# A hybrid diffusion layer: the second feed-forward product's operands pair by pair, context stores on GpSimd's queue, late residuals, and last sums of squares on TensorE

## The chip, the cores and the metric

The kernel runs on one core of one Trainium2 chip. The metric is the device time of one execution in microseconds (us). TensorE multiplies matrices; VectorE, ScalarE and GpSimd work on tiles elementwise; SyncE issues most of the DMAs. TensorE runs at one of two granted clocks, 1.2 or 2.4 GHz, which the profile shows as .50 and 1.00.

## The reference

One layer of a diffusion trunk with 256 context tokens and 1024 latent tokens, of width 1024, then a last RMSNorm. Three token mixers (a chunked state space scan, a spatial gate, a complex diagonal scan) are followed by the feed-forward part, which is the part that the change touches:

```
h = rmsnorm(x, norm1_g) * (1 + scale1) + shift1
x = x + gate1 * (concat(mixers(h @ w_in)) @ w_out)
h = rmsnorm(x, norm2_g) * (1 + scale2) + shift2                  # the "second norm"
x = x + gate2 * (square(relu(h @ ffn_w1)) @ ffn_w2)              # first and second product
y = rmsnorm(x, final_norm_g)                                     # the "last norm"
```

It is done for the context with modulation `c_ctx` and for the latents with `c`. `ffn_w1` is 1024 x 4096, `ffn_w2` 4096 x 1024, all in float32.

## The kernel before

Activations lie with features on partitions and tokens in columns: columns 0 to 255 are the context, 256 to 1279 the latents. A float32 factor is split into a high part (rounded, by ScalarE) and a low part (the rest, by VectorE), and a product is three matmuls: high x high, high x low, low x high. In the second product those are lines L1405, L1406, L1407 (`mm2`). Helpers record their own lines: L48 is every DMA, L54 every elementwise operation of two tiles, L57 every scalar-tensor-tensor operation, L60 every activation, L201 the passes with a vector of ones that sum squares over partitions, L206 the passes that spread the result.

The 4096 hidden features are 16 pairs of 256. In the first product, pairs are worked off one by one; the context's part of the last four pairs (12 to 15) is done alone at the end (`ctx_pair`): 24 matmuls of 128x256 for each of two halves, relu and square by ScalarE into `cc`, and a store to `ac_d` that ScalarE's queue issues. The latents' activations were stored to `a_d` before.

The second product then runs over groups of pairs: (0-3), (4-7), (8, 9), (10-13). It is a scheme of seven block products (`seven(i, ...)`, in the order 1, 2, 5, 6, 3, 7, 4) for the latents, and four context products `ctx2` between them. A `seven` fills four PSUM banks of tag "w" (five exist), 12 matmuls of 128x512 for each of four pairs: 48 by four banks, bank after bank. Its operands: `uA` is a weight block (from `h0`/`h1`, loads of `ffn_w2`, or from `cb`, a sum of weight blocks that GpSimd makes), `uB` an activation block (from `tb`, a load of `a_d`); `ch` and `cl` are the parts of the context activations `rc`. `tb`, `rc`, `cb` and `xt` share one ring "tm" of ten tiles. `flush` puts a bank into `X` or adds it, the last group also folds the seven X tiles into X2 to X5, which become the four quarters of the result, and applies `residual`: load `xt`, the residual stream, and y = gate x y + xt. `cacc` holds the context's sum and gets its residual likewise.

Pairs 14 and 15 come last, in `last_block` for columns 768, 1024, 256, 512, 0 in this order: eight row blocks, each 12 matmuls of 128x256 in a bank of "w", and then y = gate x bank + y by VectorE. After each block but the first, `final_norm` of the block before runs, and the one of columns 0 to 255 stands at the very end.

The order of instructions on each engine is fixed when the program is built, by a scheduler that simulates times; DMAs are issued by SyncE's queue in that order, but for the stores to `ac_d`. A DMA also waits for the one eight before it in a rotation of semaphores that SyncE's and ScalarE's DMAs share.

## Time and profile before

| | |
|---|---|
| median of 3 runs | 1550.88 us (1548.78 to 1554.53) |
| the profiled execution | 1554.11 us |
| its span, first to last instruction | 1552.3 us |
| mean granted clock of TensorE | .951 |

All times of single instructions below are us from the start of the span of the profiled execution. A row of the timeline gives start, duration, engine, line, operation, output and inputs, shape, the number of like instructions merged into it, and in brackets the idle time of the engine before it and what ended that. Matmuls overlap in the pipeline, so their pace is read from the distance of their starts, not from their durations.

### The profile page before, as it was taken

The numbers are of one execution on the slowest core, as the hardware profiler recorded it, in microseconds if no ns is written. First come the engines' busy times: TensorE is split into PE (matmuls) and PEld (weight loads), VectorE is DVE, ScalarE is ACT, GpSimd is POOL, SyncE is SP. The second block draws the span as 40 slices with busy tenths as digits, with TensorE's granted clock in tenths as the row PEclk, the third lists the DMA queues.
The fourth block names the chain that finished last, engine by engine and source line by source line (L and its number), as shares of the span: only waits on it lengthen the run. The fifth ranks groups of instructions, "written<-read, shape, count | busy, mean of one in ns | idle before, by whom it ended". The sixth has DMA issues, their size and how long they took to land.

```text
span 1552.3 us, 23665 instructions
## 1 busy us (share of the span) xinstructions
PE 1416.1 (91%) x8360; PEld 1198.5 (77%) x8360; DVE 1040.4 (67%) x1772; ACT 713.1 (46%) x1459; POOL 448.6 (29%) x527
## 2 busy tenths in 40 slices
PE   4689898899896799989999999999899999999795
PEld 3567677778774588778888888888788888887795
DVE  5773358766757854758877756574655678879945
ACT  3643434355734633447555545455555243323322
POOL 4555556734635512312000000000331403032033
PEclk9699899999998889989999999999999999999897
DMA  9758785275878874346444444345653245316312
GB/s 318 254 172 257 217 284 186 88 182 153 242 199 242 241 248 126 102 137 200 140 148 147 146 138 139 117 153 176 213 183 115 80 150 175 108 55 193 107 41 97
DMA packets 244747, 258.62 MB, mean 167 GB/s; under 512 B 16212, under 2 KB 168980, under 8 KB 244628
## 3 DMA queue, kind: packets, MB, share of 16 engines
q1 hardware_dynamic: 228724, 239.84, 50.0%
q10 hardware_dynamic: 15904, 17.27, 3.5%
q8 instruction: 66, 1.08, 0.3%
q14 instruction: 53, 0.43, 0.1%
HBM read 188.07 MB, written 68.98 MB: 166 GB/s over the span
## 4 chain that ended last, share of the span: by engine, by line
PE 63%; DVE 8%; DMA 5%; issue 3%; POOL 2%; ACT 2%; SPq 0%; DVEq 0%; ACTq 0%; POOLq 0%
PE ps_w L1251 7%; PE ps_w L1249 7%; PE ps_w L1250 7%; PE ps_w L1405 6%; PE ps_w L1406 6%; PE ps_w L1407 6%; PE ps_mm L222 5%; PE ps_mm L220 5%; PE ps_mm L221 5%; DVE X L54 2%; PE ps_mm L1406 1%; PE ps_mm L1407 1%; PE ps_mm L1405 1%; DVE uA L54 1%; POOL Ht L54 1%
## 5 line engine op out<-in xcount | busy, mean ns | idle before, releaser
L220 PE MATMUL ps_mm<-hi,wh 128*128 128x512 f32 (+1 forms) x576 | 212.6, 369 | 14.9 <-DVE dtr L708 14.5
L221 PE MATMUL ps_mm<-lo,wh 128*128 128x512 f32 (+1 forms) x576 | 211.5, 367 | 0.0
L222 PE MATMUL ps_mm<-hi,wl 128*128 128x512 f32 (+1 forms) x576 | 210.1, 365 | 0.9 <-DVE wl L54 0.9
L1406 PE MATMUL ps_w<-uB,uA 128*128 128x512 f32 (+1 forms) x520 | 191.4, 369 | 8.9 <-DVE uB L54 8.9
L1405 PE MATMUL ps_w<-uB,uA 128*128 128x512 f32 (+1 forms) x520 | 190.8, 371 | 9.0 <-ACT uB L60 8.9
L1407 PE MATMUL ps_w<-uB,uA 128*128 128x512 f32 (+1 forms) x520 | 190.5, 367 | 0.0
L54 POOL TENSOR_TENSOR cb<-h 128x512 f32<-128x512 f32 x14 | 21.7, 1559 | 513.8 <-DMA h<-w 435.1
L220 PEld LDWEIGHTS ps_mm<-hi,wh 128*128 128x128 f32 x576 | 112.2, 195 | 32.2 <-DVE dtr L708 15.3
L222 PEld LDWEIGHTS ps_mm<-hi,wl 128*128 128x128 f32 x576 | 111.7, 194 | 17.7 <-DVE wl L54 1.8
L221 PEld LDWEIGHTS ps_mm<-lo,wh 128*128 128x128 f32 x576 | 112.2, 195 | 15.2 <-issue 0.8
L1406 PEld LDWEIGHTS ps_w<-uB,uA 128*128 128x128 f32 x520 | 100.0, 192 | 25.7 <-DVE uB L54 11.0
L1405 PEld LDWEIGHTS ps_w<-uB,uA 128*128 128x128 f32 x520 | 100.0, 193 | 25.4 <-ACT uB L60 9.3
L1407 PEld LDWEIGHTS ps_w<-uB,uA 128*128 128x128 f32 x520 | 99.9, 192 | 15.6
L54 DVE TENSOR_TENSOR uB<-tb,uB 128x512 fp32r<-128x512 f32 x106 | 89.2, 864 | 12.8 <-ACT uB L60 12.8
L60 ACT ACTIVATE uB<-tb 128x512 fp32r<-128x512 f32 x106 | 65.9, 626 | 65.2 <-DMA tb<-a_d 32.4
L54 DVE TENSOR_TENSOR X<-X,ps_w 128x512 f32<-128x512 f32 x84 | 56.2, 682 | 27.7 <-PE ps_w L1407 27.6
L54 DVE TENSOR_TENSOR q<-q,ps_w 128x512 f32<-128x512 f32 x48 | 32.9, 686 | 60.4 <-PE ps_w L1251 59.6
L54 POOL TENSOR_TENSOR sg<-rb,cap 128x512 f32<-128x512 f32 x40 | 57.4, 1454 | 37.5 <-PE ps_wb L926 21.7
L60 ACT ACTIVATE c<-c 128x512 f32<-128x512 f32 x64 | 40.3, 629 | 56.6 <-DVE c L54 55.6
L54 DVE TENSOR_TENSOR wl<-wraw,wh 128x1024 fp32r<-128x1024 f32 x32 | 46.8, 1464 | 28.0 <-ACT wh L60 27.7
L1406 PE MATMUL ps_mm<-cl,uA 128*128 128x256 f32 x224 | 63.3, 283 | 0.0
L1407 PE MATMUL ps_mm<-ch,uA 128*128 128x256 f32 x224 | 63.2, 283 | 0.0
(445 smaller groups left out, 3851.9 us busy)
## 6 DMA issues: line engine op xcount, KB each, us to landing
rw<-w SPq DMA_DIRECT2D x112, 256.0 KB
tb<-a_d SPq DMA_DIRECT2D x106, 256.0 KB
aw<-ada_w SPq DMA_DIRECT2D x64, 256.0 KB
h<-w SPq DMA_DIRECT2D x32, 512.0 KB
a_d<-t SPq DMA_DIRECT2D x42, 256.0 KB
rb<-rows_d SPq DMA_DIRECT2D x20, 512.0 KB
adaw<-ada_w SPq DMA_DIRECT2D x32, 256.0 KB
wraw<-w_out SPq DMA_DIRECT2D x16, 512.0 KB
```

Source lines behind the costliest of these rows:

```text
L54: eng.tensor_tensor(out=out, in0=a, in1=b, op=op)
L60: S.activation(out=out, in_=in_, func=func, **kw)
L220: T.matmul(out, lhsT=wh(k), rhs=xh(k), start=(k == 0), stop=False)
L221: T.matmul(out, lhsT=wh(k), rhs=xl(k), start=False, stop=False)
L222: T.matmul(out, lhsT=wl(k), rhs=xh(k), start=False, stop=(k == nk - 1))
L1249: T.matmul(out, lhsT=wh, rhs=X[0][:, j, :], start=(j == 0), stop=False)
L1250: T.matmul(out, lhsT=wh, rhs=X[1][:, j, :], start=False, stop=False)
L1251: T.matmul(out, lhsT=wl, rhs=X[0][:, j, :], start=False, stop=(j == 3))
L1405: T.matmul(out, lhsT=wh, rhs=bh, start=start, stop=False)
L1406: T.matmul(out, lhsT=wh, rhs=bl, start=False, stop=False)
L1407: T.matmul(out, lhsT=wl, rhs=bh, start=False, stop=stop)
```

## The change

Five edits.

1. `norm2_stats` for the last tile of columns: the squares of k = 6 and 7 are no longer added by GpSimd but go into TensorE's sum over partitions as matmuls of their own.
2. The context parts that are done alone store to `ac_d` by GpSimd's queue; for the last pair, relu and square are VectorE's, a maximum and a product.
3. In each group the first loads of `tb` and `h0` alternate pair by pair, and so do the splits of the first operands.
4. In the last group, the residuals of X2, X4 and `cacc` and the fold of X7 into X4 are written after the first and second last block instead of inside the group.
5. `final_norm` of the last block: all eight squares go into TensorE's sum, VectorE's seven additions are gone.

```diff
     def norm2_stats(t):
         t0, n = TILES[t]
-        tot = None
+        tot = []
         for k in range(KD):
             sq = ph("sq")[:, :n]
             act(sq, acc_at(k, t), ACT.Square)
-            if k:
-                tt(tot, tot, sq, ALU.add, G)
+            if k == 0 or (t == 2 and k > 5):
+                tot.append(sq)
             else:
-                tot = sq
-        return rows_rstd([tot], n, D)
+                tt(tot[0], tot[0], sq, ALU.add, G)
+        return rows_rstd(tot, n, D)
...
-    def ctx_half(p, i, W):
+    def ctx_half(p, i, W, eng=None):
         o = proj_tile(0, W)
         c = ph("cc")[:, 0:256]
-        act(c, o, ACT.Relu)
-        act(c, c, ACT.Square)
-        load(ac_d[p][:, i, :], c, nc.scalar)
...
+        if eng and p == NPAIR - 1:
+            V.tensor_scalar(out=c, in0=o, scalar1=0.0, scalar2=None, op0=ALU.max)
+            tt(c, c, c, ALU.mult)
+        else:
+            act(c, o, ACT.Relu)
+            act(c, c, ACT.Square)
+        load(ac_d[p][:, i, :], c, eng or nc.scalar)
...
         if alone:
-            ctx_pair(p, raws)
+            ctx_pair(p, raws, nc.gpsimd)
...
-        w0 = [w2_raw(p, 0) for p in pairs]
-        tb = [act_raw(p, 0) for p in pairs]
+        w0, tb = [], []
+        for p in pairs:
+            tb.append(act_raw(p, 0))
+            w0.append(w2_raw(p, 0))
...
-        a11 = [hl_of(W(q, 0, 0), "uA") for q in Q]
-        b11 = [hl_of(z, "uB") for z in tb]
-        seven(1, a11, b11, first)
         if first:
             cacc[0] = f2.tile([128, 8, 256], F32, name="cacc")
+        a11, b11 = [], []
+        for q in Q:
+            a11.append(hl_of(W(q, 0, 0), "uA"))
+            b11.append(hl_of(tb[q], "uB"))
+        seven(1, a11, b11, first)
...
-        seven(2, a12, b21, first, [(2, 1), (2, None)] if last else ())
+        seven(2, a12, b21, first, [(2, 1)] if last else ())
         ctx2(0, 1, a12, C, False)
-        if last:
-            for m in range(4):
-                residual(cacc[0][:, m, :], m, 0)
...
-        seven(4, a22, B, first, [(4, 7), (4, None)] if last else ())
+        seven(4, a22, B, first)
         ctx2(1, 1, a22, C, False)
-        if last:
-            for m in range(4):
-                residual(cacc[0][:, 4 + m, :], 4 + m, 0)
...
             act(sq[:, k], ypos(k, t0, 256), ACT.Square)
-            if last and k:
-                tt(sq[:, 0], sq[:, 0], sq[:, k], ALU.add)
-            elif k % 2:
+            if k % 2 and not last:
                 tt(sq[:, k - 1], sq[:, k - 1], sq[:, k], ALU.add, G)
         r = f2.tile([128, 256], F32, tag="r", name="r", bufs=1)
-        S.copy(r, rows_rstd([sq[:, k] for k in ((0,) if last else range(0, KD, 2))], 256, D))
+        S.copy(r, rows_rstd([sq[:, k] for k in range(0, KD, 1 if last else 2)], 256, D))
...
         last_block(t0)
+        if i == 0:
+            for m in range(4):
+                residual(Xs[2][:, m, :], m, 1)
+            for m in range(4):
+                tt(Xs[4][:, m, :], Xs[4][:, m, :], Xs[7][:, m, :], ALU.add)
+                residual(Xs[4][:, m, :], 4 + m, 1)
+        if i == 1:
+            for m in range(8):
+                residual(cacc[0][:, m, :], m, 0)
```

What the scheduler makes of it is read from the order of the two programs. SyncE's queue at the start of the second product, before (`rw` are weights of the first product, an `h` followed by a number is a load of `ffn_w2`):

```order
L48 DMA rw<-w 128x4x128 x4
L48 DMA h_10692<-w 128x2x512
L48 DMA h_10694<-w 128x2x512
L48 DMA h_10696<-w 128x2x512
L48 DMA h_10698<-w 128x2x512
L48 DMA tb<-a_d 128x512 x4
L48 DMA h_10708<-w 128x2x512
L48 DMA h_10710<-w 128x2x512
L48 DMA h_10712<-w 128x2x512
L48 DMA h_10714<-w 128x2x512
L48 DMA rc<-ac_d 128x512 x4
```

SyncE's queue at the same place, after:

```order
L48 DMA rw<-w 128x4x128 x4
L48 DMA tb<-a_d 128x512
L48 DMA h_10700<-w 128x2x512
L48 DMA tb<-a_d 128x512
L48 DMA h_10704<-w 128x2x512
L48 DMA tb<-a_d 128x512
L48 DMA h_10708<-w 128x2x512
L48 DMA tb<-a_d 128x512
L48 DMA h_10712<-w 128x2x512
L48 DMA h_10714<-w 128x2x512
L48 DMA h_10716<-w 128x2x512
```

The four weight loads and the four activation loads now alternate; the stores of `cc`, which shared the rotation of semaphores with them, are in GpSimd's queue. The same holds for the splits on VectorE, after (before, eight `uA` low parts came first and four of `uB` then; `uubl` belongs to the first product):

```order
L54 TENSOR_TENSOR uubl<-rw,uubh 128x512 x2
L1257 TENSOR_SCALAR cc<-ps_mm 128x256
L54 TENSOR_TENSOR cc<-cc 128x256
L1257 TENSOR_SCALAR cc<-ps_mm 128x256
L54 TENSOR_TENSOR cc<-cc 128x256
L54 TENSOR_TENSOR uB<-tb,uB 128x512
L54 TENSOR_TENSOR uA<-h_10700,uA 128x512
L54 TENSOR_TENSOR uB<-tb,uB 128x512
L54 TENSOR_TENSOR uA<-h_10704,uA 128x512
L54 TENSOR_TENSOR uB<-tb,uB 128x512
L54 TENSOR_TENSOR uA<-h_10708,uA 128x512
```

The last pair's relu and square stand ahead of all of them. TensorE takes the 48 matmuls of this first `seven` pair by pair over the four banks in the program after; in the other groups it keeps its order. On ScalarE three of the copies out of these banks now stand before the first `ch`.

SyncE's queue from the last group to the end, before (the `xt` of 128x512 are those of X tiles, the ones of 128x256 those of `cacc`):

```order
L48 DMA xt<-x_d 128x512 x3
L48 DMA xt<-x_d 128x256 x4
L48 DMA tb<-a_d 128x512 x12
L48 DMA xt<-x_d 128x512 x4
L48 DMA h_14014<-w 128x2x512
L48 DMA h_14016<-w 128x2x512
L48 DMA tb<-a_d 128x512 x4
L48 DMA xt<-x_d 128x512 x4
L48 DMA tb<-a_d 128x512 x4
L48 DMA xt<-x_d 128x512 x4
L48 DMA xt<-x_d 128x256 x2
L48 DMA h_14030<-w 128x2x512
```

The end of SyncE's queue, after:

```order
L48 DMA xt<-x_d 128x512 x4
L48 DMA h_13968<-w 128x2x512
L48 DMA h_13970<-w 128x2x512
L48 DMA tb<-a_d 128x512 x4
L48 DMA xt<-x_d 128x512 x4
L48 DMA tb<-a_d 128x512 x4
L48 DMA rc<-ac_d 128x512 x2
L48 DMA tb<-a_d 128x512 x4
L48 DMA h_13984<-w 128x2x512
L48 DMA tb<-a_d 128x512
L48 DMA h_13986<-w 128x2x512
L48 DMA tb<-a_d 128x512 x3
```

Behind the last of these rows come 16 `xt` loads, eight of 128x512 and eight of 128x256, and then the output stores only; ahead of the first stand 12 `tb` loads with no `xt` before them. VectorE at the end of the last group, before (X_11055 and X_11249 are X5 and X3, X_11499 is X4):

```order
L54 TENSOR_TENSOR cacc<-cacc,ps_mm 128x512
L57 SCALAR_TENSOR_TENSOR cacc<-cacc,mod,xt 128x256 x2
L54 TENSOR_TENSOR cl<-rc,ch 128x512
L57 SCALAR_TENSOR_TENSOR X_11499<-X_11499,mod,xt 128x512
L54 TENSOR_TENSOR uA<-h_14030,uA 128x512
L54 TENSOR_TENSOR cl<-rc,ch 128x512
L54 TENSOR_TENSOR uA<-h_14032,uA 128x512
L57 SCALAR_TENSOR_TENSOR cacc<-cacc,mod,xt 128x256 x2
L54 TENSOR_TENSOR uA<-h_14032,uA 128x512
L54 TENSOR_TENSOR uB<-tb,uB 128x512 x8
L57 SCALAR_TENSOR_TENSOR X_11249<-ps_w,mod,X_11249 128x256 x4
```

VectorE there, after (X_11255 is X3, X_11505 is X4):

```order
L54 TENSOR_TENSOR cacc<-cacc,ps_mm 128x512
L54 TENSOR_TENSOR cl<-rc,ch 128x512
L57 SCALAR_TENSOR_TENSOR cacc<-cacc,mod,xt 128x256
L54 TENSOR_TENSOR uA<-h_13984,uA 128x512
L57 SCALAR_TENSOR_TENSOR X_11505<-X_11505,mod,xt 128x512
L54 TENSOR_TENSOR cl<-rc,ch 128x512
L57 SCALAR_TENSOR_TENSOR X_11255<-ps_w,mod,X_11255 128x256
L54 TENSOR_TENSOR uA<-h_13986,uA 128x512 x2
L57 SCALAR_TENSOR_TENSOR X_11255<-ps_w,mod,X_11255 128x256
L57 SCALAR_TENSOR_TENSOR X_11505<-X_11505,mod,xt 128x512
L57 SCALAR_TENSOR_TENSOR X_11255<-ps_w,mod,X_11255 128x256
```

All eight `uB` parts of pairs 14 and 15 stand earlier in the program after, the last three residuals of X4 stand among the bank reads of the first block, and seven of the eight residuals of `cacc` between its fourth and fifth bank read. The four residuals of X2, the four sums of X7 into X4 and one residual of X4 and of `cacc` stand ahead of the blocks.

## Rows read from the trace of the kernel before

**Rows 1.** The page, its first section: busy us of each engine.

```profile
PE 1416.1 (91%) x8360; PEld 1198.5 (77%) x8360; DVE 1040.4 (67%) x1772; ACT 713.1 (46%) x1459; POOL 448.6 (29%) x527
```

**Rows 2.** Windows; columns: stretch, length, busy by engine, PE clock, DMA share, GB/s.

```profile
1350.00:1375.00 25.00, 25.00 (x135) 21.65 (x134) 14.36 (x21) 3.47 (x7) 5.27 (x4) 1.00 0.02 6
...
1425.00:1450.00 25.00, 25.00 (x135) 21.67 (x134) 25.00 (x42) 8.72 (x15) 0.00 (x0) 1.00 0.43 129
...
1475.00:1500.00 25.00, 25.00 (x212) 25.00 (x211) 11.35 (x20) 6.35 (x18) 6.32 (x8) 1.00 0.07 21
```

**Rows 3.** Timeline of TensorE at the start of the second product.

```profile
1098.43 2.07 PE L1405 MATMUL ps_w<-uB,uA 128*128 128x512 f32 x4 [6.11 <-ACT uB L60]
...
1106.24 0.39 PE L1406 MATMUL ps_w<-uB,uA 128*128 128x512 f32 x1
...
1112.13 0.28 PE L1405 MATMUL ps_mm<-ch,uA 128*128 128x256 f32 x1
```

**Rows 4.** Waits of SyncE's queue, 1060 to 1110: total us, times, longest.

```profile
SPq L48 <- DMA ac_d<-cc: 16.0, 7, 5.5
```

**Rows 5.** Timeline of SyncE's queue at the start of the second product.

```profile
1080.19 8.02 SPq L48 DMA_DIRECT2D h<-w  x4
1089.42 7.46 SPq L48 DMA_DIRECT2D tb<-a_d  x4
```

**Rows 6.** Timeline of ScalarE at the same place.

```profile
1093.59 4.27 ACT L60 ACTIVATE uA<-h 128x512 fp32r<-128x512 f32 x8 [0.40 <-ACT cc L60]
...
1111.09 0.57 ACT L1413 COPY X<-ps_w 128x512 f32<-128x512 f32 x1
```

**Rows 7.** Waits of SyncE's queue in the last group, 1330 to 1420.

```profile
SPq L48 <- DVE X L57: 29.9, 2, 27.6
```

**Rows 8.** Waits of TensorE from 1300 to 1480.

```profile
PE ps_w L1406 <- DVE uB L54: 8.9, 5, 5.3
PE ps_w L1405 <- ACT uB L60: 2.8, 1, 2.8
```

**Rows 9.** Timeline of TensorE: fifth product's start, blocks 768 and 1024.

```profile
1382.96 0.86 PE L1405 MATMUL ps_w<-uB,uA 128*128 128x512 f32 x3
...
1458.63 1.03 PE L1405 MATMUL ps_w<-uB,uA 128*128 128x256 f32 x5 [2.78 <-ACT uB L60]
...
1477.88 0.28 PE L1405 MATMUL ps_w<-uB,uA 128*128 128x256 f32 x1
```

**Rows 10.** Timeline of VectorE in the last group.

```profile
1383.01 0.88 DVE L57 SCALAR_TENSOR_TENSOR cacc<-cacc,mod,xt 128x256 f32<-128x256 f32 x2
...
1385.78 2.96 DVE L57 SCALAR_TENSOR_TENSOR cacc<-cacc,mod,xt 128x256 f32<-128x256 f32 x2
...
1464.17 4.91 DVE L54 TENSOR_TENSOR uB<-tb,uB 128x512 fp32r<-128x512 f32 x8
```

**Rows 11.** Timeline of GpSimd beside the second of these.

```profile
1384.02 5.86 POOL L54 TENSOR_TENSOR cb<-cb,h 128x512 f32<-128x512 f32 x4 [8.10 <-DVE cacc L57]
```

**Rows 12.** Timeline of TensorE in the tail, sums of squares.

```profile
1530.61 1.84 PE L201 MATMUL ps_ad<-ones,fin 128*128 128x1 f32 x16
...
1541.43 1.01 PE L201 MATMUL ps_ad<-ones,fin 128*128 128x1 f32 x4 [7.72 <-DVE fin L54]
```

**Rows 13.** Timelines of ScalarE and VectorE in the tail, squares and additions.

```profile
1534.15 2.56 ACT L60 ACTIVATE fin<-cacc 128x256 f32<-128x256 f32 x8
...
1537.78 3.59 DVE L54 TENSOR_TENSOR fin<-fin 128x256 f32<-128x256 f32 x7
```

**Rows 14.** Windows in the tail and after the second norm.

```profile
1535.00:1540.00 5.00, 0.00 (x0) 0.00 (x0) 4.58 (x10) 2.90 (x9) 1.78 (x3) 0.50 0.54 184
...
675.00:681.00 6.00, 5.35 (x24) 5.04 (x25) 2.86 (x5) 2.67 (x5) 0.00 (x0) 0.51 1.14 295
```

**Rows 15.** Timeline of TensorE at the second norm of the last tile.

```profile
673.75 1.59 PE L201 MATMUL ps_ad<-ones,sq 128*128 128x1 f32 x8 [2.91 <-POOL sq L54]
...
675.99 0.58 PE L220 MATMUL ps_mm<-hi,uuah 128*128 128x256 f32 x1 [0.65 <-ACT uuah L60]
```

More of the change, by code (lines that the diff above doesn't have):

```diff
@@ L1251, in prod, with ctx_pair @@
             T.matmul(out, lhsT=wl, rhs=X[0][:, j, :], start=False, stop=(j == 3))
-    def ctx_half(p, i, W):
+    def ctx_half(p, i, W, eng=None):
         o = proj_tile(0, W)
         c = ph("cc")[:, 0:256]
-        act(c, o, ACT.Relu)
-        act(c, c, ACT.Square)
-        load(ac_d[p][:, i, :], c, nc.scalar)
-    def ctx_pair(p, raws):
+        if eng and p == NPAIR - 1:
[5 more added lines that the diff above has]
+        load(ac_d[p][:, i, :], c, eng or nc.scalar)
+    def ctx_pair(p, raws, eng=None):
         for i, tag in enumerate(("ua", "ub")):
-            ctx_half(p, i, unit(pr, tag + "h", tag + "l", 1, raws[i]))
+            ctx_half(p, i, unit(pr, tag + "h", tag + "l", 1, raws[i]), eng)
     def w1_raws(p, new):
```

## The prediction

> **What bounds the kernel now.** First the totals: TensorE is busy 1416.1 us of the span of 1552.3, VectorE 1040.4 [rows 1]. So the span is TensorE's, and a gain has to come out of TensorE's idle time and of its time at half clock; there are three such places in the stretch that the change touches. Then the tables of 25 us: in 1350 to 1375 VectorE works 14.36 us of 25, in 1425 to 1450 all 25.00 beside a full TensorE, in 1475 to 1500 11.35 [rows 2]. VectorE is thus a second bound in the last group alone, with room before and after it. Last the waits and single instructions of each place.
>
> *Start of the second product.* TensorE's first matmul of it begins at 1098.43 after 6.11 idle, so the context matmuls ended at 1092.32; its first four take 2.07 (.52 each), later ones are (1112.13 - 1106.24)/26 = .2265 apart, and the 48 of the first product end at 1112.13 [rows 3]. At .2265 they would take 10.9 and end at 1103.2: the place loses 8.9 us, 6.1 idle and the rest at half clock. Cause: SyncE waited 16.0 us, in seven waits, for context stores [rows 4], its four h loads spread over 8.02 us from 1080.19 and the four tb loads over 7.46 from 1089.42 [rows 5]; and ScalarE makes all eight uA parts (4.27 us, .53 each) from 1093.59 before any uB part [rows 6].
>
> *Last group.* SyncE waited 27.6 us in one wait for a residual (L57 into X) [rows 7]: the xt loads of X2's residuals hold the ring "tm", and the tb loads behind them are the operands of the next products. TensorE then waited 8.9 us for low parts of uB, 5.3 the longest, and 2.8 for a high part [rows 8]. From 1382.96 to 1455.85 (1458.63 less 2.78) five products and two context products took 72.9 [rows 9]; 240 x .2265 + 96 x .118 (25 us for 212 [rows 2]) = 65.7, so 7.2 lost. The block of columns 768 then lasts to 1477.88 [rows 9], 22.0 for 96 x .118 = 11.3: 10.7 lost. Together 17.9. VectorE there: a pair of cacc residuals takes .88 alone but 2.96 beside GpSimd's cb sums [rows 10, 11], and the eight last uB parts take 4.91 (.61 each) from 1464.17 [rows 10], to 1469.1.
>
> *Tail.* Sixteen passes with ones at full clock take 1.84 (.115 each), four at half clock 1.01 (.25) [rows 12]. The eight squares run 1534.15 to 1536.7, and seven VectorE additions of 3.59 follow from 1537.78, behind the normed outputs of the block before [rows 13]; the four passes then stand at 1541.43 after 7.72 idle [rows 12], and the clock is .50 in 1535 to 1540 [rows 14].
>
> **The change part by part.** *Context stores by GpSimd, operands pair by pair.* By the order SyncE's first eight loads no longer stand on stores that ScalarE issues: they need slots whose loads landed long before, so they go out from about 1078; even at the spacing of [rows 5], 2 us each, the first two pairs have landed by 1092. ScalarE, which loses relu and square of the last pair's two halves, can make uB and uA before TensorE's end instead of from 1093.59. At the head of VectorE's queue the second half waits for TensorE's end at 1092.32; behind it stand all low parts. Its two operations on 128x256 are not in the trace: bounds .3 and .6 each (half a .61 part; a whole one); I take .45, so it ends at 1093.2, the first uB and uA parts (.61 each) at 1094.4, and TensorE flows from 1094.0, its first hi x hi matmuls done before. Per pair 12 x .2265 = 2.7 us of matmul stand against 1.2 of VectorE, so the rest is covered: end 1094.0 + 10.9 = 1104.9. A new bubble follows: four banks end together, and ScalarE copies three of them (.57 each [rows 6]) before the first ch, then VectorE makes cl: 2.2 us. So the context product begins at 1107.1 instead of 1112.13: **gain 5.0**. Bounds: 7.2 without the bubble; 2 if stores from GpSimd's queue, which issues none in the trace, cost time, or the clock falls in the pause of 1.7 us as it fell in the one of 6.1.
> Of these stores the trace shows that who issues them decides when SyncE's loads go out [rows 4]. The Trainium skill (Trainium Kernel Development and Optimization, Key Constraints) says that queues of SyncE, ScalarE and GpSimd run on the same 16 DMA engines, and issuing from several saves only the issue time. By that the loads would stay spread to 1097, the third pair would come about 1 us late, and the total would be 1531 instead of 1530; the row decides.
>
> *Residuals of the last group.* Out of VectorE's stretch 1383.0 to 1469.1 (86.1 us [rows 10]) go four pairs of cacc residuals, 3 x .88 + 2.96 = 5.6, and three of the four X4 residuals, at about .8 each (a pair of half size takes .88) 2.4; the four X2 residuals, which stood before 1383, move into it, 3.2, since the scheduler puts them, the four X4 sums and one residual back ahead of the blocks. More counts what SyncE now issues ahead: the tb loads of the fifth product need buffers of uB parts done long before, and VectorE can use its idle 25 - 14.36 = 10.6 us of 1350 to 1375 [rows 2]. It can use none of it or all; I take 7, as cb sums and matmul results still set some of its order. So VectorE's last operand comes at 1383.0 + 86.1 - 5.6 - 2.4 + 3.2 - 7 = 1457.3, and TensorE, unhindered, would run the block from 1383.0 + 65.7 = 1448.7 to 1460.0 and want that operand (uA, last pair, second half) some 3 us before its end: just in time. GpSimd's cb sums still slow the low parts. I leave 3.4 of the 17.9 for waits and the clock: **gain 14.5**; bounds 17.9 and, with nothing ahead, 4.8 (rival 1). The deferred work, 3 X4 and 7 cacc residuals, 6 us, lies in blocks where VectorE is free for 13.6 of 25 us [rows 2]: nothing. SyncE is moved past it too: all 16 late xt loads stand behind the blocks' tb loads, and behind them only the output stores.
>
> *Last norm.* Seven additions go; 32 passes come. The last square ends at 1536.7; at .115 the last of eight passes of one column and sixteen of the other end at 1538.8 against 1542.44: 3.6. At .25, 16 passes paced from 1534.5 end at 1538.5 and the rest at 1542.5: nothing. The clock is .50 there [rows 14], and the start's matmuls ran long at half clock after their idle time too [rows 3], so I lean to the low end: **gain 1.0**.
> The Trainium skill (TensorE: Matmul & The Clock Gate, Part 1) states that an idle TensorE falls to half rate and has to be busy again before the full rate returns; this speaks against moving sums there. The row of .50 agrees. By the rule alone the term is 0 and the total 1531.
>
> *Second norm.* GpSimd loses two additions, TensorE's passes go from 8 to 24 (8 took 1.59, .2 each [rows 15]). They can begin about one addition sooner (1.47, of the four in [rows 11]), at 672.3; the next matmul waits for ScalarE's uuah until 675.99 anyway [rows 15]. At .2 they take 4.8 and end 1.1 too late; at .115 they end at 675.1, and if that also holds the clock, which is .51 in 675 to 681 [rows 14], up to 2.4 come back. I take 0, bounds a gain of 2.4 and a loss of 1.1.
>
> Sum: 5.0 + 14.5 + 1.0 + 0 = 20.5. The profiled execution took 1554.11 (span 1552.3), so 1533.6 there; from the median of the runs, 1550.88, **1530**.
>
> **The rivals.** (1) *VectorE stays the bound in the last group.* If cb sums on GpSimd, ScalarE's order or the matmul results keep it from working ahead, only 5.6 + 2.4 - 3.2 = 4.8 of the 17.9 come back: 1550.9 - 5.0 - 4.8 - 1.0 = 1540. For it: VectorE is full for 50 us there; against it: the 10.6 idle us just before, and the 27.6 wait of SyncE that goes.
> (2) *The start gives back what it gains*: the wait at the head of VectorE's queue, the bubble and GpSimd's stores leave 1 of 5: 1534.
> (3) *All covers hold*: no wait in the last group (17.9), the clock up in the tail (3.6): 1550.9 - 5.0 - 17.9 - 3.6 = 1524.
> (4) *Slower: the late residuals shut the PSUM banks.* In VectorE's order ten residuals stand among its reads of the first block's banks, and each waits for an xt load at the end of SyncE's queue. Five banks are full after five of 8 row blocks, 7 us; then TensorE stops. Should a wait such as the 27.6 of [rows 7] return, the price is 27.6, less the 20.5: 1558. It decides above 20 us. Against it: those loads take buffers that the last uB parts free in a row, with nothing else queued.
> (5) *The change does not do what it says*: the scheduler puts nearly all back into the group and waits remain; start and tail stay: 1545.
>
> **How the numbers follow.** The forecast, 1526 to 1537, gets .53, rival 1 .18, rival 2 (within that range) .12, rival 3 .09, rival 4 .04, rival 5 .04. The range goes from 1523 to 1543: it takes in rivals 1 to 3, leaves out 4, 5 and the ends of the unknown costs. Half a per cent, 7.8 us, is about what a measurement of this kernel tells from no change: faster is below 1543.1. Rival 1 lies near that bound, I put a quarter of it beyond. So faster .53 + .13 + .12 + .09 = .87; same .05 + .04 = .09; slower .04.
>
> **What would show it.** Start: the first four matmuls of the second product within 2 us of 1092.3, tb and h loads issued by 1085, and 2 us idle before its first context product; a pause of 5 would make the step wrong. Last group: the wait of SyncE for L57 gone, TensorE's waits for uB under 3 us instead of 11.7, the block of 768 in 11 to 14 us; VectorE full to the end with TensorE waiting would be rival 1. Blocks: TensorE without a wait for a bank. Tail: 32 passes beginning some 20 us earlier than before, the last within 4.5 us of the first if the clock is up, 8 if not. A total over 1543 would make the prediction wrong, and so would a gain that lies elsewhere than at these places.

## The result and the profile after

The changed kernel takes 1537.14 us (median of 7 runs, 1527.66 to 1540.61) against 1551.21 (7 runs, 1548.78 to 1557.45): a ratio of .9895 of the means (the medians give .9909), 95% interval .9868 to .9922. That is 14.1 us by the medians, 12.1 to 20.5 by the interval; 20.5 were forecast. The profiled execution took 1540.37 us, its span is 1538.6, its mean granted clock .957.

Where the time went is read from TensorE's starts in the two profiled executions. "Late part" is all from the end of the context matmuls done alone to the end of the span: the stretch with edits 2 to 5. Each column is one execution.

| stretch, us | before | after | gain | forecast |
|---|---|---|---|---|
| to the end of the context matmuls done alone | 1092.2 | 1095.8 | -3.6 | 0 (edit 1) |
| start: to the second context product | 36.8 | 33.6 | 3.1 | 5.0 |
| middle: to the fifth product of the last group | 254.0 | 254.0 | 0 | 0 |
| last group: five products, two context products | 72.9 | 66.0 | 6.9 | |
| block 768 | 22.0 | 14.1 | 7.9 | 14.5, with the group |
| block 1024 | 13.2 | 14.7 | -1.4 | 0 |
| last three blocks | 39.5 | 39.5 | 0 | 0 |
| tail, from the last block's end | 21.7 | 20.9 | .8 | 1.0 |
| late part | 460.1 | 442.8 | 17.3 | 20.5 |

*Start.* TensorE (timeline of after; columns as in [rows 3]) begins the second product at once, and meets three short waits where [rows 3] had one of 6.11:

```profile
1095.77 0.40 PE L1409 MATMUL ps_w<-uB,uA 128*128 128x512 f32 x1
...
1097.51 0.50 PE L1410 MATMUL ps_w<-uB,uA 128*128 128x512 f32 x1 [1.34 <-DVE uB L54]
...
1109.73 0.50 PE L1409 MATMUL ps_mm<-ch,uA 128*128 128x256 f32 x2 [1.27 <-ACT ch L60]
...
1112.37 0.58 PE L1410 MATMUL ps_mm<-cl,uA 128*128 128x256 f32 x1 [0.93 <-DVE cl L54]
```

The context product thus starts 13.96 us after the matmuls done alone (1109.73 - 1095.77), 6.0 sooner than before (1112.13 - 1092.17 = 19.96), but then loses 2.9 of that. The windows (columns as in [rows 2]) show the half clock behind the last wait, the timeline of VectorE the slow `cl` parts ahead of it, and the head of its queue:

```profile
1112.00:1114.00 2.00, 1.63 (x7) 1.63 (x8) 2.00 (x3) 1.80 (x4) 1.60 (x1) 0.50 0.05 9
1114.00:1116.00 2.00, 2.00 (x11) 1.86 (x10) 2.00 (x4) 0.00 (x0) 0.07 (x1) 0.70 0.61 147
```

```profile
1095.97 0.42 DVE L1257 TENSOR_SCALAR cc<-ps_mm 128x256 f32<-128x256 f32 x1 [1.95 <-PE ps_mm L222]
1096.43 0.42 DVE L54 TENSOR_TENSOR cc<-cc 128x256 f32<-128x256 f32 x1
1096.77 0.69 DVE L54 TENSOR_TENSOR uB<-tb,uB 128x512 fp32r<-128x512 f32 x1
...
1109.71 0.69 DVE L54 TENSOR_TENSOR cl<-rc,ch 128x512 fp32r<-128x512 f32 x1 [5.63 <-ACT ch L60]
1110.72 3.89 DVE L54 TENSOR_TENSOR cl<-rc,ch 128x512 fp32r<-128x512 f32 x3 [0.32 <-ACT ch L60]
```

SyncE's first eight loads, four `tb` and four `h`, went out from 1081.27 to 1086.3 (timeline of its queue; the last of the eight is the first of the five `h` at 1085.62, the others are second weight halves). That is 9.4 us ahead of TensorE's end at 1095.77, where the forecast had 1085 for an end at 1092.3, and they take 5.1 us where [rows 5] had 16.7. No wait for a store is left:

```profile
1081.27 0.46 SPq L48 DMA_DIRECT2D tb<-a_d  x1
...
1083.85 1.10 SPq L48 DMA_DIRECT2D h<-w  x1
1085.00 0.58 SPq L48 DMA_DIRECT2D tb<-a_d  x1
1085.62 5.13 SPq L48 DMA_DIRECT2D h<-w  x5
1091.33 4.23 SPq L48 DMA_DIRECT2D rc<-ac_d  x4
```

*Last group.* TensorE's waits of 1300 to 1480 (total, times, longest), to be set beside [rows 8]: those for `uB` are gone, and what is left is in blocks 768 and 1024.

```profile
PE ps_w L1409 <- DVE X L57: 2.3, 2, 1.3
PE ps_w L1411 <- DVE uA L54: 1.0, 1, 1.0
```

These are three single waits in TensorE's timeline; VectorE's timeline shows the last `uA` parts at 1456.23 and 1458.49, and, behind four bank reads with residuals of X4 among them, the seven `cacc` residuals in one piece ahead of the reads of five full banks (L57, X from `ps_w`):

```profile
1456.96 0.38 PE L1411 MATMUL ps_w<-uB,uA 128*128 128x256 f32 x1 [1.03 <-DVE uA L54]
...
1458.62 0.39 PE L1409 MATMUL ps_w<-uB,uA 128*128 128x256 f32 x1 [1.04 <-DVE X L57]
...
1466.74 0.39 PE L1409 MATMUL ps_w<-uB,uA 128*128 128x256 f32 x1 [1.29 <-DVE X L57]
```

```profile
1456.23 0.68 DVE L54 TENSOR_TENSOR uA<-h,uA 128x512 fp32r<-128x512 f32 x1
...
1458.49 1.28 DVE L54 TENSOR_TENSOR uA<-h,uA 128x512 fp32r<-128x512 f32 x2
...
1462.95 3.34 DVE L57 SCALAR_TENSOR_TENSOR cacc<-cacc,mod,xt 128x256 f32<-128x256 f32 x7
1466.21 2.04 DVE L57 SCALAR_TENSOR_TENSOR X<-ps_w,mod,X 128x256 f32<-128x256 f32 x5
```

*Tail and second norm.* The 32 passes stand where [rows 12] had a pause of 7.72 and four passes; the whole time that they take they run at half clock. At the second norm, 20 passes run at full clock, 1.16 us behind the first four, and the fall comes after them (timeline of TensorE, then windows):

```profile
1521.67 6.99 PE L201 MATMUL ps_ad<-ones,fin 128*128 128x1 f32 x32 [0.91 <-ACT fin L60]
```

```profile
675.09 2.39 PE L201 MATMUL ps_ad<-ones,sq 128*128 128x1 f32 x20 [1.16 <-ACT sq L60]
```

```profile
1522.00:1525.00 3.00, 3.00 (x16) 3.00 (x15) 2.92 (x5) 2.96 (x9) 1.85 (x3) 0.50 0.25 86
1525.00:1529.00 4.00, 3.66 (x18) 3.58 (x17) 0.00 (x1) 0.26 (x1) 0.00 (x0) 0.50 0.59 197
```

```profile
674.20:678.20 4.00, 2.39 (x20) 2.31 (x20) 0.18 (x1) 0.93 (x2) 0.00 (x0) 1.00 0.72 220
678.60:680.00 1.40, 1.40 (x5) 1.18 (x6) 1.21 (x2) 0.78 (x2) 0.00 (x0) 0.50 0.91 240
680.00:685.00 5.00, 5.00 (x25) 5.00 (x25) 1.62 (x4) 1.26 (x2) 0.00 (x0) 0.50 1.13 288
```

### The profile page after: what moved, and what is told of

Same layout as the page of the kernel before. It is cut to its first block, busy times and chain, and to the rows that moved or that the text cites. A ratio compares the mean times of both kernels' runs of the same rounds, so it can differ in the third digit from the quotient of the medians.

```text
span 1538.6 us, 23751 instructions
## 1 busy us (share of the span) xinstructions
PE 1416.1 (92%) x8404; PEld 1202.5 (78%) x8404; DVE 1035.3 (67%) x1769; ACT 709.6 (46%) x1455; POOL 454.8 (30%) x533
## 4 chain that ended last, share of the span: by engine, by line
PE 71%; DVE 13%; DMA 8%; POOL 3%; issue 3%; ACT 2%; SPq 1%; DVEq 0%; ACTq 0%; POOLq 0%
PE ps_mm L220 7%; PE ps_mm L222 7%; PE ps_mm L221 7%; PE ps_w L1251 7%; PE ps_w L1249 7%; PE ps_w L1250 7%; PE ps_w L1409 6%; PE ps_w L1410 6%; PE ps_w L1411 6%; DVE lo L57 2%; PE ps_mm L1410 2%; PE ps_mm L1411 2%; PE ps_mm L1409 1%; DVE X L54 1%; POOL Ht L54 1%
## 5 line engine op out<-in xcount | busy, mean ns | idle before, releaser
L1409 PE MATMUL ps_w<-uB,uA 128*128 128x512 f32 (+1 forms) x520 | 189.0, 364 | 2.3 <-DVE X L57 2.3
L1410 PE MATMUL ps_w<-uB,uA 128*128 128x512 f32 (+1 forms) x520 | 189.0, 363 | 1.3 <-DVE uB L54 1.3
L1411 PE MATMUL ps_w<-uB,uA 128*128 128x512 f32 (+1 forms) x520 | 186.5, 363 | 1.0 <-DVE uA L54 1.0
L220 PEld LDWEIGHTS ps_mm<-hi,wh 128*128 128x128 f32 x576 | 110.7, 192 | 34.6 <-DVE dtr L708 16.8
L1409 PEld LDWEIGHTS ps_w<-uB,uA 128*128 128x128 f32 x520 | 98.2, 189 | 17.4 <-DVE X L57 2.6
L1411 PEld LDWEIGHTS ps_w<-uB,uA 128*128 128x128 f32 x520 | 98.0, 189 | 16.6 <-DVE uA L54 1.2
L1410 PEld LDWEIGHTS ps_w<-uB,uA 128*128 128x128 f32 x520 | 98.2, 189 | 16.3 <-DVE uB L54 1.7
L48 POOL DMA_DIRECT2D ac_d<-cc x8 | 4.5, 563 | 354.2 <-ACT cc L60 350.4
```

The costliest lines, as they stand in the source:

```text
L220: T.matmul(out, lhsT=wh(k), rhs=xh(k), start=(k == 0), stop=False)
L1409: T.matmul(out, lhsT=wh, rhs=bh, start=start, stop=False)
L1410: T.matmul(out, lhsT=wh, rhs=bl, start=False, stop=False)
L1411: T.matmul(out, lhsT=wl, rhs=bh, start=False, stop=stop)
```

## The experiments

The first 1084 to 1096 us differ between executions by more than most of the terms, and edits 2 to 5 don't touch them. So each kernel's late part is compared as well as its time.

| kernel | us | runs | late part | start | products | block 768 | tail |
|---|---|---|---|---|---|---|---|
| before | 1551.2 | 7 | 460.1 | 36.8 | 72.9 | 22.0 | 21.7 |
| after | 1537.1 | 7 | 442.8 | 33.6 | 66.0 | 14.1 | 20.9 |
| e1_group: edit 4 alone | 1536.6 | 4 | 446.1 | 35.9 | 66.0 | 15.6 | 21.9 |
| e2_start: edits 2, 3 | 1547.5 | 10 | 455.2 | 32.4 | | | 21.8 |
| e3_norms: edits 1, 5 | 1547.9 | 10 | 458.1 | 36.9 | | | 20.9 |
| e5_stores: edit 2 alone | 1548.0 | 1 | 458.3 | 34.9 | | | 21.7 |
| e6_pairs: edit 3 alone | 1548.1 | 1 | 458.4 | 35.2 | | | 21.7 |
| e7_x2back: edit 4, X2's kept | 1535.5 | 1 | 446.4 | 35.6 | 66.0 | 15.8 | 22.2 |
| e8_x2only: X2's alone moved | 1548.4 | 1 | 451.6 | 36.0 | 66.1 | 21.1 | 21.7 |
| e10_noload | 1537.4 | 1 | 446.2 | 35.9 | 66.0 | 15.3 | 22.2 |
| e12_unread | 1534.3 | 1 | 448.2 | 36.8 | 66.0 | 16.8 | 21.9 |
| e4_early | 1524.6 | 4 | 436.8 | | 66.0 | 14.1 | 21.0 |
| e9_blocks | 1527.1 | 4 | 434.5 | | 66.0 | 11.5 | 21.0 |
| e11_sums | 1519.0 | 4 | 426.0 | | 66.0 | 11.6 | 16.5 |

The kernel before ran beside them at medians of 1548.3 to 1548.5 (its single run beside e12_unread: 1549.6). Kernels that are alike at a place differ there too, from one profiled execution to another: the start takes 35.6 to 36.9 us in the seven without edits 2 and 3, products and block 768 together 93.5 to 94.9 in the five with all residuals where they were, the tail 21.7 to 22.2 in the nine without edit 5.

**Which edits bring it.** e1_group leaves only edit 4 in the kernel, e2_start only edits 2 and 3, e3_norms only edits 1 and 5.

> The kernel before with edit 4 alone (residuals of the last group deferred). Theory (each edit acts at its own place and the gains add up): from the first matmul of the fifth product of the last group to the first of the third late block, 108.2 us before, falls to 94.7 as with all edits; the start of the second product (36.8 us from the last context matmul of the first product to the second context product) and the tail stay; total 1551 - 13.5 = 1537.5. Rival (the last group gains only because operands are early from the start on): the stretch falls by less than 8 and TensorE still waits over 5 us for low parts of uB; total above 1543.

> The kernel before with edits 2 and 3 alone (context stores by GpSimd, last pair's relu and square by VectorE, first operands pair by pair). Theory: the start stretch of 36.8 us falls to 33.7 as with all edits, with 1.3 us idle before the second matmul and about 2.4 us idle and a spell of half clock around the first context product; the last group stays at 108; total 1551 - 3 = 1548. Rival (the order earns more than the trace of the whole change shows, because its stretch was disturbed there): 31.5 or less, total 1546.

> The kernel before with edits 1 and 5 alone (squares summed by TensorE in the second and the last norm). Theory (matmuls of one column do not bring the clock back): the tail from the first sum of squares of the block before last to the end falls from 21.7 to 20.9, its 32 passes run at about .22 us each at clock .50; after the second norm the first product begins no earlier and stays at half clock as long or longer, 1 us lost; total 1551, within 1 us of before. Rival (the added passes hold the clock): passes of .115, tail 18, nothing cold after the second norm, total 1545.

Measured against before: .9928 (.9900 to .9956), .9992 (.9972 to 1.0012), .9991 (.9969 to 1.0013). Edit 4 alone gives 14.0 us in the late part, most of the 17.3; edits 2 and 3 give 4.3 at their place (3.2 to 4.5 against the range above), the norms .8 in the tail, and both stay below what the whole time can show. In e2_start TensorE has the very same three waits at the start as in after (1.3, 1.3, 1.2 in all), but the clock stays up behind them, and the stretch is 1.2 us shorter than in after:

```profile
1105.00:1107.00 2.00, 1.72 (x13) 1.73 (x14) 2.00 (x3) 1.70 (x4) 1.68 (x1) 1.00 0.08 15
```

In block 768 e1_group has VectorE's order of after and the same two waits (1.02 and 1.04 us), but slow clock behind them, where after has none. Its block 768 is 1.5 us longer than that of after and its block 1024 1.4 shorter, the two together 28.8 us against 28.7: where the loss falls is luck of the clock, and VectorE, which reads the first full banks 8.7 us behind the block's start in either, sets the end (windows, e1_group first, then after):

```profile
1455.00:1458.00 3.00, 2.39 (x13) 2.39 (x13) 3.00 (x7) 0.83 (x2) 0.32 (x1) 0.67 0.30 91
1458.00:1461.00 3.00, 3.00 (x21) 3.00 (x21) 3.00 (x6) 1.24 (x3) 1.15 (x2) 0.76 0.00 0
```

```profile
1455.00:1458.00 3.00, 1.55 (x11) 1.15 (x10) 3.00 (x6) 0.00 (x0) 0.00 (x0) 1.00 0.29 84
1458.00:1461.00 3.00, 2.38 (x20) 2.38 (x21) 3.00 (x7) 0.84 (x2) 0.31 (x1) 1.00 0.31 91
```

**Which of the two start edits.** e5_stores is before with edit 2, e6_pairs before with edit 3.

> The kernel before with edit 2 alone. The scheduler leaves the order of loads and splits as before: all uA parts ahead of the uB parts. Theory (the order of splits carries the start's gain, the stores' engine only sets when loads go out): SyncE's 16 us of waits for context stores vanish, its first loads are out by 1085, but VectorE still makes eight low parts of uA before the first of uB; the start stretch is about 35 us against 36.8 before. Rival (the loads were what the start waited for): 33 or less.

> The kernel before with edit 3 alone (loads and splits pair by pair, context stores still in ScalarE's queue). Theory: SyncE's waits for context stores stay, the loads stay spread over some 15 us, and TensorE flows about 1 us later than with edits 2 and 3, ScalarE being held by the last pair's relu and square: start stretch 33.5 to 34.5. Rival (loads spread so far leave the third and fourth pair late): 36 or more, with a wait of over 2 us for uB inside the first product.

The start is 1.9 and 1.6 us shorter than in the one execution of before, .7 to 2.0 and .5 to 1.8 against the range of the kernels without these edits, so the waits say more than the sizes: each edit removes one of two walls. With the stores moved, TensorE still waits for all `uA` parts to be made ahead of the first `uB`; with the pairs alternating, SyncE still waits for the stores (waits of TensorE in e5_stores, of SyncE's queue and of TensorE in e6_pairs):

```profile
PE ps_w L1409 <- ACT uB L60: 4.8, 1, 4.8
```

```profile
SPq L48 <- DMA ac_d<-cc: 16.5, 6, 4.5
...
PE ps_w L1405 <- ACT uA L60: 2.5, 1, 2.5
```

**What of the residuals cost the products.** e7_x2back is edit 4 with X2's residuals left in the group; e8_x2only moves these alone, the first against e1_group:

```diff
-        seven(2, a12, b21, first, [(2, 1)] if last else ())
+        seven(2, a12, b21, first, [(2, 1), (2, None)] if last else ())
...
```

The loop for X2 behind the first block is gone there too.

> Edit 4 alone, but with the four residuals of X2 left inside the last group, so that their four xt loads stand ahead of the tb loads of the fifth product again. Theory (the group waited because those tb loads stood behind xt loads in SyncE's queue): five products and two context products take 70 or more (72.9 before, 66.0 with edit 4), with TensorE waiting for low parts of uB; the stretch to the third late block 99 or more. Rival (VectorE's amount of work was the limit, and the work that is still deferred is enough): 66 to 67 and 96 or less.

> The kernel before with the four residuals of X2 alone deferred, the other residuals where they were. Theory (queue): the products of the last group take 66 to 68, but the blocks of columns 768 and 1024 stay late by VectorE's work: stretch to the third late block 100 to 103. Rival (amount of work): little changes, 106 or more.

Either half of the residuals may stay: the products take 66.0 and 66.1 us. So X2's loads alone are not what held the operands, as the prediction read it from [rows 7]; eight such loads together are. Block 768 takes 21.1 us in e8_x2only and 15.8 in e7_x2back, but this isn't the amount of VectorE's work ahead of it: the two kernels below leave all of that work in and take 15.3 and 16.8. In e8_x2only the four X2 residuals, whose loads are the last that SyncE issues there, stand ahead of and among the reads of the first banks, and TensorE waits 3.33 us for a bank, with the clock at .50 behind it, 1466 to 1469 (timelines of VectorE and TensorE):

```profile
1463.39 1.41 DVE L57 SCALAR_TENSOR_TENSOR X<-X,mod,xt 128x512 f32<-128x512 f32 x2
1464.71 0.88 DVE L57 SCALAR_TENSOR_TENSOR X<-ps_w,mod,X 128x256 f32<-128x256 f32 x2
```

```profile
1465.25 0.58 PE L1405 MATMUL ps_w<-uB,uA 128*128 128x256 f32 x1 [3.33 <-DVE X L57]
```

Two more kernels, both otherwise the kernel before, part the eight residuals of X2 and of the first half of the context into work, transfer and held buffer:

```diff
         xt = tm("xt")[:, :n]
         load(xt, x_d[m][:, t0:t0 + n])
-        stt(y, y, gate2[:, m, s:s + 1], xt, ALU.mult, ALU.add)
+        late = t == 1 and m < 4 or t == 0 and m < 4
+        stt(y, y, gate2[:, m, s:s + 1], y if late else xt, ALU.mult, ALU.add)
```

This is e12_unread; e10_noload leaves out `xt` and `load` for these eight too.

> The kernel before, with one thing left out: the X2 residuals and the first four context residuals of the last group do the same VectorE operation on the same tiles, but take the product itself in place of the residual stream, so that eight loads are gone and no work of an engine (the residual stream isn't added there). If the eight loads in SyncE's queue and ring were what lost 7 us in the last group's products (72.7 us before, 66.0 with either half of them deferred): 66 to 67 us, and TensorE's waits for uB in 1300 to 1480 us fall from 11.7 to under 3 us. If the VectorE work itself lost them: 71 to 73 us and the waits stay. Both halves of it: between 68 and 70.

> The kernel before, with the same eight residuals as in the run without their loads (X2's four and the first four of the context) again taking the product itself in place of the residual stream, but with their loads left in: the same transfers stand in SyncE's queue in the same order and into the same buffers, only that VectorE no longer reads them, so a buffer comes free when its transfer has landed and not when VectorE has come to the residual. The residual stream is left out there. Without the loads the last group's products took 66.0 us against 72.9. Theory that the buffers are held until VectorE's residual, and that the loads of the operands behind them wait for that: 66 to 67 us again, and SyncE's longest wait for a residual, 27.6 us before, is under 20. Rival, that the transfers themselves or the buffers that they take, held or not, delay the operands: 71 to 73 us as before. Half of each: 68 to 70.

Both give 66.0 us, and TensorE's waits for `uB` fall from 11.7 us to 1.3 and 1.2. With the same operations on VectorE, and in e12_unread with the same order and the same transfers in SyncE's queue, the loss is gone once a buffer comes free when its transfer has landed. VectorE's order is not the same: in e12_unread four `uB` parts made from the loads behind the `xt` stand at 1351.5 to 1354.5, ahead of X2's residuals; before, the first of them stands at 1381.7, behind these. SyncE's queue (timeline; before first, then e12_unread, whose stretch to the second context product ended about 8 us sooner):

```profile
1331.43 18.12 SPq L48 DMA_DIRECT2D xt<-x_d  x7
1377.29 23.28 SPq L48 DMA_DIRECT2D tb<-a_d  x12
```

```profile
1323.58 9.81 SPq L48 DMA_DIRECT2D xt<-x_d  x7
1333.48 45.13 SPq L48 DMA_DIRECT2D tb<-a_d  x12
```

Before, eight of the ten tiles of "tm" wait for VectorE's residuals, the queue stands, and the first of twelve `tb` loads goes out at 1377; in the other it goes out right behind the `xt` loads. So the cause is held buffers in front of a queue that works in order, not traffic and not the amount of VectorE's work. VectorE's other order isn't parted from it by a run; alone it could not have helped before, since these loads had not gone out.

**What is left at the start and in the blocks.** e4_early has edits 2 to 5, loads `rc` ahead of the second half of the weights in the first group, and makes the context's residual inside its own last block, the last of all (shown against after; the loop for it behind the second block is gone):

```diff
+        if first:
+            C = [ctx_unit(p) for p in pairs]
         w1 = [w2_raw(p, 1) for p in pairs]
...
-            stt(y, o, gate2[:, m, s:s + 1], y, ALU.mult, ALU.add)
+            if t0 < NCTX:
+                tt(y, y, o, ALU.add)
+                residual(y, m, 0)
+            else:
+                stt(y, o, gate2[:, m, s:s + 1], y, ALU.mult, ALU.add)
```

> All edits but edit 1, and two changes: in the first group the context activations are loaded ahead of the second weight halves, so that ScalarE and VectorE split them before the copies out of the first four banks; and the context residuals are added in the last block itself, after its sum, so that they cannot be put ahead of the earlier blocks' bank reads. Theory (the shortfall against the forecast is the wait for ch and cl with the half clock that follows, the seven context residuals ahead of bank reads, and the second norm): start stretch 33.7 to about 30.5, late block 1024 14.7 to 13.3, late block 768 14.1 to 13.5, second norm 1 back, tail .4 more; total 5 us less than with the whole change, 1532. Rival (the copies that now come after the splits hold the banks, so that the wait only moves to the second product): start stretch 33 or more, total 1535 or more.

It takes .9852 of before (.9827 to .9878; after .9868 to .9922), with a late part 6.0 us under that of after. At the start one of the three waits is left, 1.34 for `uB`, and the clock holds: the start and the middle together take 283.2 us, 7.6 less than before (after: 3.1 less). Block 1024 is back at 13.0 us. e9_blocks does the same with the residuals of columns 256 and 512 (against e4_early; their loops behind the first block are gone):

```diff
-            if t0 < NCTX:
+            if t0 < 768:
                 tt(y, y, o, ALU.add)
-                residual(y, m, 0)
+                xt = tm("xt")[:, :256]
+                load(xt, x_d[m][:, t0:t0 + 256])
+                stt(y, y, gate2[:, m, s:s + 1], xt, ALU.mult, ALU.add)
```

> As the early loads (edits 2 to 5, the context loads ahead of the weights, the context residual inside its own last block), and now the residuals of the other two late blocks (columns 256 and 512) are also applied inside their own last blocks, 256 columns at a time, so that VectorE folds nothing but banks between the last products and block 768. Theory that the two late residuals hold VectorE ahead of block 768 (after: 14.08 us for that block against 13.0 to 13.2 for the next ones): block 768 takes 12 to 13 us, nothing else changes, total 1 to 2 us under the early loads, 1522 to 1524. Rival, that the added VectorE work in the later blocks holds their banks: block 768 is shorter but the three blocks behind it take 13.5 us or more each, total the same or above. Rival, that block 768 waits for something else than VectorE: 14 us again.

Block 768 falls from 14.1 to 11.5 us, its 96 matmuls at .12 apart and nothing else; TensorE waits for nothing from 1300 to 1500, and the later blocks keep their time (39.5). The late part is 2.3 us under that of e4_early; the time of the whole kernel is 2.5 above, .9856 (.9827 to .9884), with overlapping intervals and a beginning 2.3 us longer in the profiled execution. So the place is settled; a gain in the whole time is not shown.

**What the sums cost.** e11_sums is e9_blocks with all sums of the last norms as matmuls with ones on 256 columns; the squares are written in the rounded form that TensorE reads in one pass (eight matmuls leave eight records in the trace, where the 16 float32 ones of after leave 32). The main part against e9_blocks:

```diff
-            if k % 2 and not last:
-                tt(sq[:, k - 1], sq[:, k - 1], sq[:, k], ALU.add, G)
...
-        S.copy(r, rows_rstd([sq[:, k] for k in range(0, KD, 1 if last else 2)], 256, D))
+        p = bank("ad", 1)[:, :256]
+        for k in range(KD):
+            T.matmul(p, lhsT=onesr[:, 0:1].to_broadcast([128, 128]), rhs=sq[:, k], start=(k == 0), stop=(k == KD - 1))
+        rstd(p, r, D)
```

> As the blocks' residuals kernel, and all sums of squares of the final norms made by eight TensorE matmuls of 128x256 against a broadcast matrix of ones, with the squares written in the form that TensorE reads in one pass: the sum then stands on all partitions, GpSimd adds nothing and the one-column sums, the copies and the passes that spread the result are gone. Theory that those one-column passes cost TensorE their own time (32 of them took 6.99 us in the tail after the change, and 16 or more stand in every later block): the three later blocks take 12.2 to 12.6 us instead of 13.2, and the tail falls from 20.9 to 15 to 17 us; total 6 to 9 us under the blocks' residuals kernel. Rival, that the tail is set by the chain of square, sum, root, scaling and store and not by the passes: the tail falls by under 3 us and the total by under 5. Rival, that the root and the reciprocal over 128x256 on VectorE instead of few columns take the gain: the tail stays at 20 us or more.

1518.96 us, .9806 of before (.9777 to .9835), the fastest kernel here. Four blocks with a sum in or behind them lose .9, 1.3, 1.3 and .5 us, the tail 4.5: 8.4 in all. TensorE's timeline and a window of the tail; the eight passes are as long as the eight squares that feed them (2.55 on ScalarE), and the clock is up:

```profile
1501.28 2.53 PE L1552 MATMUL ps_ad<-fin,onesr 128*128 128x256 f32 x8 [0.92 <-ACT fin L60]
```

```profile
1501.20:1503.90 2.70, 2.53 (x8) 1.48 (x8) 2.66 (x3) 2.70 (x10) 1.11 (x2) 1.00 0.00 0
```

Both rivals fall: the passes take 2.53 us instead of 6.99, which is 4.46 of the tail's 4.5, and the reciprocal over 128x256 (1.75 us) takes less than the gain. What the root and the reciprocal over 256 columns cost, and what the copies and spreading passes gave back, no run parts. The chain now has another limit: the passes end at 1503.8, but the root waits until 1506.44 for VectorE's last read of `r` by the norm of the block before (1.88 idle on ScalarE), since there is one buffer of it.

## Why the prediction was right or wrong

The forecast of 1530 was 7 us too low; the time lies in its range, and the gain lies at the places that it named, with the last group first. Of the 20.5 us, 17.3 came in the late part, 3.2 too few; the beginning was 3.6 longer in this execution, and both together are the 6.8 that it lies above 1533.6. Of the 3.6, 2.7 stand already at the end of the slab ahead of the second norm (673.19 against 670.45), where no edit has come yet; and since e3_norms, with edit 1, has the shortest beginning of all (1084.2) and e8_x2only, without it, one of the longest (1095.0), no edit is shown to cause it.

- **Start, 5.0 forecast, 3.1 measured.** The part up to the context product was right: 13.96 us against 14.8 (1107.1 - 1092.3), and the first four matmuls have started 2.3 us after the end, 1.34 of it the wait for the first low part of `uB`; the prediction's sign was 2. The step that failed is "a new bubble follows ... 2.2 us": it ended the account at the first context matmul. Behind it came .22 and .93 more for `cl`, and a spell at half clock (.50, then .70). The lower bound named that clock; e2_start shows the same waits without it and 4.3, e4_early without the bubble 7.6. The VectorE operations, bounded at .3 to .6, took .42. The `cl` parts slipped because three of them took 3.89 us beside GpSimd's `cb` sums, 1.30 each where one alone takes .69; the prediction knew this contention from [rows 10, 11] and didn't count it here. The Trainium skill (GPSIMD Engine Reference, 1. Specifications) says that GpSimd's interfaces to SBUF are shared with VectorE, with contention for VectorE instructions of two SBUF inputs; `cl` reads two, and the row agrees.
- **Who issues the stores.** The row was followed against the rule. e5_stores shows it: SyncE's 16.0 us of waits for stores go, and the start is 1.9 us shorter (.7 to 2.0 by the range above). The Trainium skill (Trainium Kernel Development and Optimization, Key Constraints) says that issuing from several engines only saves issue time; on GpSimd a store took .54 us to issue, and what was gained is that wait. The loads went out as forecast, if one counts from TensorE's end: eight of them from 14.5 to 9.4 us ahead of it, against 14.3 to 7.3 forecast; by the rule they would have stayed spread out.
- **Last group, 14.5 forecast, 13.4 measured.** VectorE's last operand was put at 1457.3 "just in time". It came at 1459.8, counted from the fifth product's start 2.0 us later than that: the wait for `uA` at 1456.96 is that lateness, and at 1458.62 TensorE waits for a bank that VectorE had not read yet (block 768: 14.1 us, the sign was 11 to 14). Two reasons were off. Of what holds the operands, "the xt loads of X2's residuals hold the ring" named too few: e7_x2back keeps these and loses nothing in the products; e10_noload and e12_unread show that eight held buffers of ten are the cause. The sign held: in the stretch of [rows 7] SyncE's longest wait for L57 falls from 27.6 us to 1.5 in after, 2.6 in e7_x2back and 2.7 in e12_unread. What stands behind such a wait decides: e9_blocks has one of 22.0 us in its last blocks (1442 to 1464), behind the last operand load, and TensorE waits for nothing. The second is the term "nothing" for the deferred work, which "lies in blocks where VectorE is free". It failed by 1.4 us: seven `cacc` residuals of 3.34 us in one piece shut the five banks in block 1024. That is rival 4's mechanism, at 1.3 us instead of 27.6, since no load was late; in e4_early it is gone. That the loss stands in block 1024 and not in block 768 is luck of the clock, as e1_group shows. The 3.4 us left for waits and clock in the group were about right (22.0 - 14.1 = 7.9 and 6.9 of a possible 17.9; 2.6 to go, which e9_blocks gets).
- **Last norm, 1.0 forecast, .8 measured.** The lean to half clock was right: 6.99 us for 32 passes, and the last within 8 us of the first, not 4.5.
- **Second norm, 0 forecast, .15 measured** (5.54 to 5.39 us from the last matmul of the slab to the next product). "If that also holds the clock" came half true: 1.00 during the 20 passes at .12 each, then .50 from 678.6 to 685, where [rows 14] had .51 from 675 to 681. The spell moved and was not saved.
- **Rivals.** Rival 1 (1540) is nearest by the time alone, but not by its mechanism: VectorE had room ahead of the group and used it, though it then still set the pace of blocks 768 and 1024. Its sign, VectorE full to the end with TensorE waiting, is there only in small: one wait of 1.03 us for `uA`, and 2.3 for banks. Rival 5 fell with the products' 66.0.

## What to carry to other kernels

When a queue works in order and its buffers come from one ring, count how many of the ring's tiles are held by work that is not urgent: half of the residuals could stay, all of them stopped the loads behind. Late elementwise work is best put where its result is read, a tile at a time between bank reads, not as one piece ahead of them. When a new wait replaces an old one, go on with the account past it: what the wait does to the clock and to the next operands was as much as half the gain.

## What was not expected of the hardware

- The 32 passes of one column in the tail of after ran at .50 from first to last, 6.99 us; the eight passes of 256 columns in e11_sums, after a pause just as long (.92 and .91), ran at 1.00 in 2.53 us and gave the spread result with them. What ran ahead of the pause differs too: one-column passes and the spreading there, eight passes of 256 columns here.
- The same three waits of 3.8 us in all brought half clock in after (.50 in 1112 to 1114) and none in e2_start (1.00 in 1105 to 1107). The two waits in block 768 of after and e1_group are a second such pair. A term that rests on the clock after a short pause has to be given both values.
- The beginning varies by 10.7 us between executions of kernels that are alike there (1084.3 in e12_unread, 1095.0 in e8_x2only). Verdicts on terms of 1 to 5 us had to come from stretches, not from the whole time.
